# First block's mixer: the second query tile's attention tail split into three heads and one, both with priority

## The chip, the cores and the metric

One Trainium2 chip; the kernel runs on one of its cores. The metric is the device time of one execution in microseconds, the median over several runs.

## The reference

The program computes two transformer blocks one after the other: `first_block` (two layers, sequence of 256 tokens behind 16 meta tokens, 272 in all, width 1024) and `second_block` (two layers, whose norms are modulated by a vector made from a conditioning input `c`). Each layer of the first block has a mixer and a feed-forward part. The mixer, cut to what matters here:

```python
hn = rms_norm(h, norm_mix_g[l])
q, k, v, xr, gate = jnp.split(hn @ w_in[l], splits, axis=-1)
...
o_attn = diff_attention(q, k, v, lam)              # 4 heads, value width 128
o_attn = (rms_norm(o_attn, subln_g[l]) * (1.0 - lam_init)).reshape(B, T, D_ATTN)
o_rec = rg_lru_branch(xr, gate, conv_w[l], ...)    # conv, two gates, linear scan, gelu(gate)
o_rec = rms_norm(o_rec, rec_norm_g[l])
h = h + jnp.concatenate([o_attn, o_rec], axis=-1) @ w_out[l]
```

In `rg_lru_branch` the scan is over `a = exp(log_a)` and `u = sqrt(max(-expm1(2 log_a), 0)) * i * xc`, where `log_a` and `i` come from two 64x64 block matrices applied to the convolved `xc` (the gates).

## The kernel before, in words

All activations of the first block stay on the chip, channels on the partitions and the 272 tokens along the row. Every large product is made of three matmuls of split operands, high part by high part (line 359), low by high (360) and high by low (361). Weights come in blocks of 512 KB on SP's DMA queue (line 331); ScalarE copies the high part (336) and VectorE subtracts it to get the low part (337), three blocks ahead of their use.

`first_mixer` (line 612) projects q and k, normalizes them, projects v, and then runs the attention. `first_attend` (line 798) is a generator: for one tile of 128 queries it makes one head per step (scores, softmax on ScalarE and VectorE, transposes of the probabilities, the matmuls with v on lines 851 and 853 into the PSUM tile `po`), and after the last head it makes the tail: squares of `po` with a row sum on ScalarE (863), a small chain of reciprocal square root on VectorE (394 to 402, 865), the multiply that gives `on` (867), four transposes into the PSUM tile `pt` (871), the high part `mh` on ScalarE (878) and the low part `ml` on VectorE (879). Tile i=2 is the meta tokens (first layer only), i=0 and i=1 are the two halves of the sequence.

Between the heads' steps the recurrent branch is issued: `taps(c)` (convolution) and `gate(c)` for four chunks c of 128 channels. A gate has two matmuls into `pt` (741), each followed by a Tanh that reads it (742), then Tanh and Exp (743, 744). When the last gate is through, VectorE clips `th` (767), ScalarE takes its square root (768, which needs another function table to be loaded), and VectorE runs `recurrence(c)` (750 to 754, the scan is 753), adding squares into `rs` (423 to 427). `rstd_row` turns `rs` into a norm factor RR (matmul 437, the chain 394 to 402, matmul 446, copy 450), and lines 775 to 777 make `mh` and `ml` of chunks 4 to 7.

The output projection (781 to 796) has two halves of four weight blocks each: half 0 reads `mh`, `ml` of chunks 0 to 3, which are the attention, half 1 those of chunks 4 to 7, which are the recurrence. Line 791 adds each result to `h`. Into half 0 the steps of `ada_step` (469 on) are woven: the product of the conditioning vector with its weights `wada` (line 482, 128x32 by 32x256, four per 512 KB block), which come on POOL's queue (480) into five buffers. In the trace such a matmul leaves two records, so "x8" on line 482 or "x2" on line 741 is four matmuls, or one.

The order on each engine is the tile scheduler's: it walks the program in the order written, and what is issued under `high_priority(n)` is moved ahead by n. Each engine then runs its list in order, so an instruction that waits holds up all that stand behind it on that engine. PSUM buffers: `PSUM_BUFS` on line 39 gives acc 3, st 1, sc 2, pt 1, po 1; `pt` is shared by the gates' matmuls, the transposes of the probabilities and those of `on`.

Of the kernel before, what the change touches and what calls it, by code (L numbers as in the profile page):

```python
# [7 lines left out]
F32 = mybir.dt.float32  # L8
F32R = mybir.dt.float32r
I32 = mybir.dt.int32  # L10
AF = mybir.ActivationFunctionType
ALU = mybir.AluOpType
# [8 lines left out]
EPS = 1e-6  # L21
# [11 lines left out]
HP = 400  # L33
# [249 lines left out]
class Net:  # L283
# [514 lines left out]
    def first_attend(self, mp, l, i, qk, vn, aq, nlam, sub, mh, ml):  # L798

        nc = self.nc  # L800
        if i < 2:
            t0, nk = TILES[i][0], TILES[i][0] + 128
            mask = (self.m1, self.m2)[i]
            units = range(4)
        else:
            t0, nk, mask, units = 0, 16, self.m0, (0,)
        po = self.psum("po")
        rr = self.sp.tile([128, 4], F32, tag="rr", name="rr")
        for h in units:
            mx = self.sp.tile([128, 2], F32, tag="mx", name="mx")  # L810
            s = self.sp.tile([128, 2], F32, tag="sm", name="sm")
            p = []
            for c in range(2):
                r = slice(64 * c, 64 * c + 64)
                ps = self.psum("sc")
                if i < 2:
                    nc.tensor.matmul(ps[:, :nk], qk["q", h][r, t0:t0 + 128], qk["k", h][r, :nk], start=True, stop=True)
                    sc = aq[:, 16 * i + 8 + 2 * h + c:16 * i + 9 + 2 * h + c]
                else:
                    for hh in range(4):  # L820
                        nc.tensor.matmul(ps[32 * hh:32 * hh + 32, :16], qk["q", hh][r, 0:32], qk["k", hh][r, :16],
                                         start=True, stop=True, tile_position=(64 * c, 32 * hh))
                    sc = aq[:, 40 + c:41 + c]
                t = mp.tile([128, T], F32, tag=f"p{c}", name="p", bufs=2)[:, :nk]
                nc.vector.tensor_tensor_reduce(t, ps[:, :nk], mask, sc, -3e38, op0=ALU.add, op1=ALU.max,
                                               accum_out=mx[:, c:c + 1])
                p.append(t)
            nm = self.sp.tile([128, 2], F32, tag="nm", name="nm")
            nc.vector.tensor_scalar(nm, mx, -1.0, None, op0=ALU.mult)
            for c in range(2):  # L830
                nc.scalar.activation(p[c], p[c], AF.Exp, bias=nm[:, c:c + 1], accum_out=s[:, c:c + 1])
            r2 = self.sp.tile([128, 2], F32, tag="r2", name="r2")
            nc.vector.reciprocal(r2, s)
            nc.vector.tensor_copy(rr[:, h:h + 1], r2[:, 0:1])
            ra = self.sp.tile([128, 1], F32, tag="ra", name="ra")
            nc.vector.tensor_tensor(ra, s[:, 0:1], r2[:, 1:2], op=ALU.mult)
            nc.vector.tensor_tensor(ra, ra, nlam, op=ALU.mult)
            nc.vector.scalar_tensor_tensor(p[0], p[1], ra, p[0], op0=ALU.mult, op1=ALU.add)
            nt = nk // 128
            pt = self.psum("pt")  # L840
            nc.tensor.transpose(pt[0:16, 0:128], p[0][:, 0:16], self.idt)
            for j in range(nt):
                nc.tensor.transpose(pt[:, 128 + 128 * j:256 + 128 * j], p[0][:, 16 + 128 * j:144 + 128 * j], self.idt)
            am = mp.tile([16, 128], F32, tag="am", name="am", bufs=2)
            nc.scalar.activation(am, pt[0:16, 0:128], AF.Copy)
            if nt:
                a = mp.tile([128, 256], F32, tag="aT", name="aT", bufs=2)
                nc.scalar.activation(a[:, :128 * nt], pt[:, 128:128 + 128 * nt], AF.Copy)
            if i < 2:
                o = po[:, 128 * h:128 * h + 128]  # L850
                nc.tensor.matmul(o, am, vn[2][0:16, h], start=True, stop=False)
                for j in range(nt):
                    nc.tensor.matmul(o, a[:, 128 * j:128 * j + 128], vn[j][:, h], start=False, stop=j == nt - 1)
            else:
                for hh in range(4):
                    nc.tensor.matmul(po[32 * hh:32 * hh + 32, 0:128], am[:, 32 * hh:32 * hh + 32], vn[2][0:16, hh],
                                     start=True, stop=True, tile_position=(0, 32 * hh))
            yield
        n = len(units)
        so = self.sp.tile([128, 4], F32, tag="so", name="so")  # L860
        for h in units:
            junk = mp.tile([128, 128], F32, tag="junk", name="junk", bufs=2)
            nc.scalar.activation(junk, po[:, 128 * h:128 * h + 128], AF.Square, scale=rr[:, h:h + 1], accum_out=so[:, h:h + 1])
        y = self.rsqrt(so[:, :n], (128, n), 1.0 / 128, EPS, "ro")
        nc.vector.tensor_tensor(y, y, rr[:, :n], op=ALU.mult)
        on = mp.tile([128, 4, 128], F32, tag="on", name="on", bufs=2)[:, :n]
        nc.vector.tensor_tensor(on, po[:, :128 * n].rearrange("p (h e) -> p h e", h=n),
                                y.rearrange("p (h o) -> p h o", o=1).to_broadcast([128, n, 128]), op=ALU.mult)
        pt = self.psum("pt")
        for h in units:  # L870
            nc.tensor.transpose(pt[:, 128 * h:128 * h + 128], on[:, h], self.idt)
        if i < 2:
            src = pt.rearrange("p (h t) -> p h t", h=4)
            d = slice(t0, t0 + 128)
        else:
            src = pt[:, :128].rearrange("p (h t) -> p h t", h=4)[:, :, 0:16]
            d = slice(0, 16)
        nc.scalar.activation(mh[:, 0:4, d], src, AF.Copy, scale=sub)
        nc.vector.scalar_tensor_tensor(ml[:, 0:4, d], src, sub, mh[:, 0:4, d].bitcast(F32), op0=ALU.mult, op1=ALU.subtract)
        yield  # L880

    def gelu2(self, pool, out, x, n):
# [649 lines left out]
```

## Time and profile before

| | |
|---|---|
| median of 3 runs | 1718.66 us (1716.64 to 1721.53) |
| profiled execution: time | 1715.54 us |
| profiled execution: span | 1713.8 us |
| TensorE busy | 1654.7 us (97%) |
| VectorE busy | 1261.8 us (74%) |
| ScalarE busy | 848.1 us (49%) |
| mean granted TensorE clock | 0.982 |

All times below are microseconds from the start of the span, which begins 1.7 us or so later than the execution's own time counts. The mixer of the first layer is at about 60 to 160 us of it, that of the second at about 415 to 510. In the chain of waits and in the timelines, a bracket behind a row tells how long the engine was idle ahead of it and what released it.

### The profile page before, as it was taken

How to read it: one execution, taken by the hardware profiler on the slowest of the kernel's cores; microseconds unless marked ns; L12 is line 12 of the kernel's file. 1: busy time of each engine (PE TensorE's matmuls, PEld its weight loads, DVE VectorE, ACT ScalarE, POOL GpSimd, SP SyncE). 2: the span in 40 equal slices, each digit the busy share in tenths (PEclk: the TensorE clock that was granted, in tenths of full speed). 3: DMA queues.
4: the chain of work that ended last, by engine and by line, in shares of the span. 5: the costliest groups of instructions: out<-in, count | busy, mean ns of one | idle time of the engine just before them, and what ended most of it. 6: DMA issues, size and time to landing. Idle time of an engine off the chain costs nothing.

```text
span 1713.8 us, 27366 instructions
## 1 busy us (share of the span) xinstructions
PE 1654.7 (97%) x10336; PEld 1407.6 (82%) x10336; DVE 1261.8 (74%) x2713; ACT 848.1 (49%) x1614; POOL 71.2 (4%) x143
## 2 busy tenths in 40 slices
PE   8999999999989999999999999899999899979998
PEld 7869999998769999996667877677887786669997
DVE  7678986675887766745548898786867977687777
ACT  5575543454756444534556543133332846665554
POOL 0011000000000000000100011010100000000000
PEclk9999999999999999999999999899999999989999
DMA  7446655564356565432223355564642321146663
GB/s 267 157 156 233 217 172 172 166 188 152 101 189 191 184 185 185 143 99 74 72 71 99 111 170 192 163 201 140 215 161 85 119 75 38 62 119 186 186 185 112
DMA packets 71851, 256.77 MB, mean 150 GB/s; under 512 B 8584, under 2 KB 8600, under 8 KB 71720
## 3 DMA queue, kind: packets, MB, share of 16 engines
q1 hardware_dynamic: 56904, 203.58, 37.6%
q0 software_dynamic: 14672, 51.45, 9.2%
q8 instruction: 81, 1.33, 0.3%
q14 instruction: 50, 0.41, 0.1%
q10 hardware_dynamic: 144, 0.00, 0.0%
HBM read 253.92 MB, written 1.07 MB: 149 GB/s over the span
## 4 chain that ended last, share of the span: by engine, by line
PE 84%; DVE 7%; issue 5%; ACT 2%; DMA 1%; POOL 0%; DVEq 0%; POOLq 0%; ACTq 0%
PE acc L359 16%; PE acc L361 16%; PE acc L360 16%; PE up L361 6%; PE up L360 6%; PE up L359 6%; PE sc L1322 3%; PE y L359 2%; PE y L361 2%; PE y L360 2%; PE po L1333 2%; PE pt L1327 2%; DVE wlo L337 2%; PE st L533 1%; DVE asum L526 1%
## 5 line engine op out<-in xcount | busy, mean ns | idle before, releaser
L336 ACT ACTIVATE whi<-raw 128x1024 fp32r<-128x1024 f32 (+2 forms) x439 | 397.4, 919 | 544.7 <-PE acc L360 240.6
L337 DVE TENSOR_TENSOR wlo<-raw,whi 128x1024 fp32r<-128x1024 f32 (+2 forms) x439 | 457.4, 1050 | 204.9 <-ACT whi L336 196.8
L359 PE MATMUL acc<-hi,whi 128*128 128x272 f32 (+1 forms) x848 | 250.3, 295 | 7.8 <-ACT hi L567 7.2
L361 PE MATMUL acc<-hi,wlo 128*128 128x272 f32 (+1 forms) x848 | 248.1, 293 | 0.8 <-DVE wlo L337 0.8
L360 PE MATMUL acc<-lo,whi 128*128 128x272 f32 (+1 forms) x848 | 247.8, 292 | 0.0
L359 PEld LDWEIGHTS acc<-hi,whi 128*128 128x128 f32 x848 | 163.4, 193 | 15.3 <-ACT hi L567 7.2
L359 PE MATMUL acc<-whi,op 128*128 128x512 f32 (+1 forms) x432 | 157.0, 364 | 8.8 <-DVE y L1271 8.4
L360 PEld LDWEIGHTS acc<-lo,whi 128*128 128x128 f32 x848 | 163.4, 193 | 1.6 <-DVE lo L568 0.3
L361 PE MATMUL acc<-op,wlo 128*128 128x256 f32 (+1 forms) x528 | 164.7, 312 | 0.0
L360 PE MATMUL acc<-op,whi 128*128 128x256 f32 (+1 forms) x528 | 164.5, 312 | 0.2 <-DVE op L1072 0.2
L359 PE MATMUL acc<-op,whi 128*128 128x256 f32 (+1 forms) x528 | 164.4, 313 | 0.3 <-ACT qraw L1467 0.3
L361 PEld LDWEIGHTS acc<-hi,wlo 128*128 128x128 f32 x848 | 163.4, 193 | 1.2 <-DVE wlo L337 0.8
L360 PE MATMUL acc<-wlo,op 128*128 128x512 f32 (+1 forms) x432 | 155.2, 360 | 0.0
L360 PE MATMUL up<-op,whi 128*128 128x512 f32 (+1 forms) x384 | 146.2, 381 | 0.0
L359 PE MATMUL up<-op,whi 128*128 128x512 f32 (+1 forms) x384 | 145.6, 381 | 0.2 <-ACT pt L1070 0.2
L361 PE MATMUL up<-op,wlo 128*128 128x512 f32 (+1 forms) x384 | 145.0, 379 | 0.1
L359 PEld LDWEIGHTS acc<-op,whi 128*128 128x128 f32 x528 | 100.0, 190 | 8.7 <-issue 2.2
L360 PEld LDWEIGHTS acc<-op,whi 128*128 128x128 f32 x528 | 101.1, 192 | 6.6 <-issue 1.1
L526 DVE SCALAR_TENSOR_TENSOR asum<-wadb,csp,asum 128x1024 f32<-128x1024 f32 x84 | 104.4, 1277 | 2.1 <-DMA wadb<-wadb 2.1
L361 PEld LDWEIGHTS acc<-op,wlo 128*128 128x128 f32 x528 | 100.1, 190 | 6.3 <-issue 2.1
L359 PEld LDWEIGHTS acc<-whi,op 128*128 128x128 f32 x432 | 82.7, 192 | 25.9 <-DVE y L1271 8.8
L360 PEld LDWEIGHTS acc<-wlo,op 128*128 128x128 f32 x432 | 82.5, 191 | 12.2 <-issue 1.0
(416 smaller groups left out, 3389.9 us busy)
## 6 DMA issues: line engine op xcount, KB each, us to landing
raw<-wts SPq DMA_DIRECT2D x362, 512.0 KB, 3.7
wadb<-wadb POOLq DMA_DIRECT2D x64, 512.0 KB, 4.4
wada<-wada POOLq DMA_DIRECT2D x27, 512.0 KB, 5.6
raw<-wts SPq DMA_DIRECT2D x8, 384.0 KB, 3.1
B<-brow SPq DMA_DIRECT2D x6, 512.0 KB, 3.3
wada<-wada SPq DMA_DIRECT2D x5, 512.0 KB, 6.5
nb<-nbias POOLq DMA_DIRECT2D x16, 128.0 KB, 2.5
h<-xm SPq DMA_DIRECT2D x4, 272.0 KB
```

Of the source, the lines that this page charges most:

```text
L336: nc.scalar.activation(hi[:, cs], raw[:, cs], AF.Copy)
L337: nc.vector.tensor_tensor(lo[:, cs], raw[:, cs], hi[:, cs].bitcast(F32), op=ALU.subtract)
L359: mm(out, a[0], b[0], start=start, stop=False)
L360: mm(out, a[0], b[1], start=False, stop=False)
L361: mm(out, a[1], b[0], start=False, stop=stop)
L526: nc.vector.scalar_tensor_tensor(acc[s], w, c, acc[s], op0=ALU.mult, op1=ALU.add)
L533: nc.tensor.matmul(ps[:, 8 * s + m:8 * s + m + 1], acc[s][:, 128 * m:128 * m + 128], self.ones[:, 0:1], start=True, stop=True)
L1322: mm(ps[i], q[a][rows[i], tok], k[b][rows[i], k0:k0 + nk], start=n == 0, stop=n == 2)
L1327: nc.tensor.transpose(pt[:, 128 * j:128 * j + 128], p[:, 128 * j:128 * j + 128], self.idt)
L1333: mm(po[rows[i]], v[k0 // 128 + j][:, vc:vc + 64], pT[i][j // 2][:, 256 * (j % 2):256 * (j % 2) + 256], start=j == 0, stop=j == nj - 1, ti ...
```

## The change

The tail of `first_attend` becomes an inner function `finish(h0, h1)` that does the same for the heads h0 to h1 - 1. For tile i=1 it is called twice: `finish(0, 3)` after the last head's matmuls with v, and `finish(3, 4)` at the end, both under `high_priority(HP)` with HP = 400. For i=0 and i=2 it is called once, as before. The squares are now on line 816, the multiply with the factor on 819, `on` on 821, the transposes on 825, `mh` on 834 and `ml` on 835.

```diff
--- before.py
+++ after.py
@@ -806,6 +806,35 @@
             t0, nk, mask, units = 0, 16, self.m0, (0,)
         po = self.psum("po")
         rr = self.sp.tile([128, 4], F32, tag="rr", name="rr")
+
+        def finish(h0, h1):
+
+            n = h1 - h0
+            so = self.sp.tile([128, 4], F32, tag="so", name="so")
+            for h in range(h0, h1):
+                junk = mp.tile([128, 128], F32, tag="junk", name="junk", bufs=2)
+                nc.scalar.activation(junk, po[:, 128 * h:128 * h + 128], AF.Square, scale=rr[:, h:h + 1],
+                                     accum_out=so[:, h - h0:h - h0 + 1])
+            y = self.rsqrt(so[:, :n], (128, n), 1.0 / 128, EPS, "ro")
+            nc.vector.tensor_tensor(y, y, rr[:, h0:h1], op=ALU.mult)
+            on = mp.tile([128, 4, 128], F32, tag="on", name="on", bufs=2)[:, :n]
+            nc.vector.tensor_tensor(on, po[:, 128 * h0:128 * h1].rearrange("p (h e) -> p h e", h=n),
+                                    y.rearrange("p (h o) -> p h o", o=1).to_broadcast([128, n, 128]), op=ALU.mult)
+            pt = self.psum("pt")
+            for h in range(n):
+                nc.tensor.transpose(pt[:, 128 * h:128 * h + 128], on[:, h], self.idt)
+            if i < 2:
+                src = pt[:, :128 * n].rearrange("p (h t) -> p h t", h=n)
+                d = slice(t0, t0 + 128)
+                hs = slice(h0, h1)
+            else:
+                src = pt[:, :128].rearrange("p (h t) -> p h t", h=4)[:, :, 0:16]
+                d = slice(0, 16)
+                hs = slice(0, 4)
+            nc.scalar.activation(mh[:, hs, d], src, AF.Copy, scale=sub)
+            nc.vector.scalar_tensor_tensor(ml[:, hs, d], src, sub, mh[:, hs, d].bitcast(F32), op0=ALU.mult,
+                                           op1=ALU.subtract)
+
         for h in units:
             mx = self.sp.tile([128, 2], F32, tag="mx", name="mx")
             s = self.sp.tile([128, 2], F32, tag="sm", name="sm")
@@ -855,28 +884,18 @@
                 for hh in range(4):
                     nc.tensor.matmul(po[32 * hh:32 * hh + 32, 0:128], am[:, 32 * hh:32 * hh + 32], vn[2][0:16, hh],
                                      start=True, stop=True, tile_position=(0, 32 * hh))
+            if i == 1 and h == 3:
+                with self.tc.high_priority(HP):
+                    finish(0, 3)
             yield
-        n = len(units)
-        so = self.sp.tile([128, 4], F32, tag="so", name="so")
-        for h in units:
-            junk = mp.tile([128, 128], F32, tag="junk", name="junk", bufs=2)
-            nc.scalar.activation(junk, po[:, 128 * h:128 * h + 128], AF.Square, scale=rr[:, h:h + 1], accum_out=so[:, h:h + 1])
-        y = self.rsqrt(so[:, :n], (128, n), 1.0 / 128, EPS, "ro")
-        nc.vector.tensor_tensor(y, y, rr[:, :n], op=ALU.mult)
-        on = mp.tile([128, 4, 128], F32, tag="on", name="on", bufs=2)[:, :n]
-        nc.vector.tensor_tensor(on, po[:, :128 * n].rearrange("p (h e) -> p h e", h=n),
-                                y.rearrange("p (h o) -> p h o", o=1).to_broadcast([128, n, 128]), op=ALU.mult)
-        pt = self.psum("pt")
-        for h in units:
-            nc.tensor.transpose(pt[:, 128 * h:128 * h + 128], on[:, h], self.idt)
         if i < 2:
-            src = pt.rearrange("p (h t) -> p h t", h=4)
-            d = slice(t0, t0 + 128)
+            if i == 0:
+                finish(0, 4)
+            else:
+                with self.tc.high_priority(HP):
+                    finish(3, 4)
         else:
-            src = pt[:, :128].rearrange("p (h t) -> p h t", h=4)[:, :, 0:16]
-            d = slice(0, 16)
-        nc.scalar.activation(mh[:, 0:4, d], src, AF.Copy, scale=sub)
-        nc.vector.scalar_tensor_tensor(ml[:, 0:4, d], src, sub, mh[:, 0:4, d].bitcast(F32), op0=ALU.mult, op1=ALU.subtract)
+            finish(0, 1)
         yield
 
     def gelu2(self, pool, out, x, n):
```

How the scheduler's lists move is shown for the second layer's mixer, at the end of its attention. First TensorE. Before, from the last head's matmul with v (853) over the last gate's two matmuls (741) to the first matmuls of the projection (359 with whi); the rows of line 482 are the conditioning vector's:

```order
L853 MATMUL po<-vn_5014,aT 128x128
L741 MATMUL pt<-xc_5738,gates 128x272
L482 MATMUL acc<-wada,cs 32x256 x8
L741 MATMUL pt<-xc_5738,gates 128x272
L482 MATMUL acc<-wada,cs 32x256 x12
L871 MATMUL pt<-con_139,on 128x128 x4
L482 MATMUL acc<-wada,cs 32x256 x4
L359 MATMUL acc<-mh,whi_5628 128x256 x2
L482 MATMUL acc<-wada,cs 32x256 x3
```

The same place in the change:

```order
L882 MATMUL po<-vn_5034,aT 128x128
L482 MATMUL acc<-wada,cs 32x256 x15
L825 MATMUL pt<-con_139,on 128x128 x3
L482 MATMUL acc<-wada,cs 32x256 x4
L359 MATMUL acc<-mh,whi_5648 128x256 x2
L482 MATMUL acc<-wada,cs 32x256
L741 MATMUL pt<-xc_5758,gates 128x272
L360 MATMUL acc<-ml,whi_5648 128x256
L361 MATMUL acc<-mh,wlo_5649 128x256
L359 MATMUL acc<-mh,whi_5648 128x256
L360 MATMUL acc<-ml,whi_5648 128x256
L361 MATMUL acc<-mh,wlo_5649 128x256
```

The last gate's first matmul moved from directly behind line 853 to behind 20 matmuls of line 482, three transposes and two matmuls of the projection; its second follows after five more of the projection (and the last head's transpose after eight). In the first layer's mixer the list has 18, 3 and 1 matmuls of line 482 at these places.

Second ScalarE, at the same place, from the last gelu of the recurrent branch to the square root. Before:

```order
L888 ACTIVATE gl<-gl 128x272
L863 ACTIVATE junk,so<-po,rr 128x128 x2
L742 ACTIVATE tr<-pt,bh 128x272
L863 ACTIVATE junk,so<-po,rr 128x128
L743 ACTIVATE th<-tr,sp_4968 128x272
L863 ACTIVATE junk,so<-po,rr 128x128
L742 ACTIVATE ti<-pt,bh 128x272
L744 ACTIVATE tr<-tr,sp_4969 128x272
L768 ACT_TABLE_LOAD
L768 ACTIVATE th<-th 128x1088
L878 ACTIVATE mh<-pt,subg 128x4x128
```

And in the change:

```order
L907 ACTIVATE gl<-gl 128x272
L816 ACTIVATE junk,so<-po,rr 128x128 x4
L834 ACTIVATE mh<-pt,subg 128x3x128
L742 ACTIVATE tr<-pt,bh 128x272
L743 ACTIVATE th<-tr,sp_4988 128x272
L742 ACTIVATE ti<-pt,bh 128x272
L744 ACTIVATE tr<-tr,sp_4989 128x272
L834 ACTIVATE mh<-pt,subg 128x128
L768 ACT_TABLE_LOAD
L768 ACTIVATE th<-th 128x1088
```

All squares and `mh` of three heads now stand ahead of the gate's Tanh, and in this layer `mh` of the last head ahead of the table load (in the first layer it stands behind the square root). On VectorE `ml` moved from behind the first product of the recurrence (line 752) to ahead of the recurrence: three heads' within the second small chain, the last head's ahead of line 750.

## Rows read from the trace of the kernel before

**Rows 1.** The page's busy times: engine, busy us, share of the span, instructions.

```profile
PE 1654.7 (97%) x10336; PEld 1407.6 (82%) x10336; DVE 1261.8 (74%) x2713; ACT 848.1 (49%) x1614; POOL 71.2 (4%) x143
```

**Rows 2.** The page's chain that ended last, by engine.

```profile
PE 84%; DVE 7%; issue 5%; ACT 2%; DMA 1%; POOL 0%; DVEq 0%; POOLq 0%; ACTq 0%
```

**Rows 3.** TensorE's waits, 112 to 150 us: total us, times, longest.

```profile
PE acc L482 <- DMA wada<-wada: 1.5, 2, 0.8
PE acc L482 <- DVE th L750: 1.3, 1, 1.3
```

**Rows 4.** TensorE's waits, 465 to 510 us.

```profile
PE acc L482 <- DMA wada<-wada: 2.9, 2, 2.7
...
PE acc L359 <- ACT mh L776: 0.7, 1, 0.7
```

**Rows 5.** TensorE's waits, 146 to 300 us.

```profile
PE acc L359 <- DVE h L791: 0.4, 1, 0.4
```

**Rows 6.** Timeline, second mixer: start, us, engine, line, operation, out<-in, count [idle before].

```profile
470.94 0.62 PE L741 MATMUL pt<-xc,gates 128*128 128x272 f32 x2
...
471.14 0.37 ACT L863 ACTIVATE junk<-po,rr 128x128 f32<-128x128 f32 x1 [0.78 <-PE po L853]
...
475.71 1.11 ACT L768 ACTIVATE th<-th 128x1088 f32<-128x1088 f32 x1
...
476.88 0.98 PE L482 MATMUL acc<-wada,cs 128*32 128x256 f32 x8 [2.67 <-DMA wada<-wada]
...
478.09 1.06 PE L482 MATMUL acc<-wada,cs 128*32 128x256 f32 x2 [0.24 <-DMA wada<-wada]
...
480.95 0.75 DVE L879 SCALAR_TENSOR_TENSOR ml<-pt,subg,mh 128x512 fp32r<-128x512 f32 x1 [2.59 <-ACT mh L878]
...
488.52 1.22 DVE L337 TENSOR_TENSOR wlo<-raw,whi 128x1024 fp32r<-128x1024 f32 x1
...
490.15 0.83 PE L437 MATMUL st<-con,rs 128*128 128x1 f32 x6
...
499.49 0.62 PE L359 MATMUL acc<-mh,whi 128*128 128x256 f32 x3 [0.67 <-ACT mh L776]
```

**Rows 7.** Timeline, first mixer.

```profile
117.46 0.62 PE L741 MATMUL pt<-xc,gates 128*128 128x272 f32 x2
...
121.14 0.17 DVE L394 TENSOR_SCALAR rv<-so 128x4 f32<-128x4 f32 x1 [0.25 <-ACT junk L863]
...
121.40 0.64 PE L482 MATMUL acc<-wada,cs 128*32 128x256 f32 x8 [0.67 <-DMA wada<-wada]
...
122.42 1.11 ACT L768 ACTIVATE th<-th 128x1088 f32<-128x1088 f32 x1
...
123.12 0.69 DVE L867 TENSOR_TENSOR on<-po,ro 128x512 f32<-128x512 f32 x1
...
125.42 1.10 PE L871 MATMUL pt<-con,on 128*128 128x128 f32 x4
...
126.56 0.69 ACT L878 ACTIVATE mh<-pt,subg 128x512 fp32r<-128x512 f32 x1 [3.03 <-PE pt L871]
...
127.28 0.75 DVE L879 SCALAR_TENSOR_TENSOR ml<-pt,subg,mh 128x512 fp32r<-128x512 f32 x1 [1.29 <-ACT mh L878]
...
136.58 0.44 DVE L791 TENSOR_TENSOR h<-h,acc 128x272 f32<-128x272 f32 x1 [0.99 <-PE acc L361]
...
137.66 0.72 PE L437 MATMUL st<-con,rs 128*128 128x1 f32 x6
...
143.84 1.35 ACT L776 ACTIVATE mh<-xc,g 128x272 fp32r<-128x272 f32 x3 [0.51 <-DVE xc L775]
...
146.59 0.37 PE L359 MATMUL acc<-mh,whi 128*128 128x272 f32 x1 [0.37 <-DVE h L791]
```

**Rows 8.** Windows: us, busy of PE, PEld, DVE, ACT, POOL, granted clock, DMA share, GB/s.

```profile
125.00:129.00 4.00, 4.00 (x22) 1.79 (x21) 2.69 (x8) 1.12 (x2) 0.53 (x1) 0.57 1.00 401
498.00:499.00 1.00, 0.66 (x4) 0.42 (x4) 1.00 (x3) 0.20 (x2) 0.31 (x1) 1.00 0.93 356
```

## The prediction

> **What bounds the kernel now.** I read the page first. Its busy line shows TensorE at work in 97% of the span [rows 1], and the chain that ended last is TensorE for 84% of it [rows 2]; look there for the one engine whose time adds up to the whole. So nothing that VectorE or ScalarE gains or loses counts unless TensorE then waits less or more. Second, TensorE's waits in the two stretches that the change touches. In the first mixer they are 1.5 us for the c-vector's weights (wada) and 1.3 us where VectorE is late [rows 3]; in the second they are 2.9 us for wada and 0.7 us for mh of line 776, the first operand of the projection's second half [rows 4]. Between 146 and 300 us TensorE waits 0.4 us in all [rows 5], so whatever TensorE loses at the first mixer's second half is not made good behind it. Third, the timelines of both stretches, to see what stands between the last gate and that second half [rows 6, 7]. There lies the argument: the second half needs the recurrence, the recurrence needs the Sqrt of line 768, and Sqrt needs the last gate's matmuls of line 741. In the second mixer TensorE already waits for the end of this chain; in the first, the first mh (a third of the 1.35 us from 143.84) is written at 144.3 and the half starts at 146.59, so there are 2.3 us of room.
>
> **What moves.** The tail's eight squares, transposes and so on stay as many; per mixer the change adds a second chain of ten small VectorE operations (the chain took 121.14 to 123.12, so 1.98 us [rows 7]), one multiply, one ml and one mh. Alone that is about 3 us of VectorE and 0.4 of ScalarE per mixer, in gaps where VectorE waits 2.59 and 1.29 us for mh [rows 6, 7]; I cost it at nothing by itself. The c-vector's matmuls, their loads on POOL's queue and the weights' loads on SP's keep their number and, but for one weight load that goes ahead of a 4 KB store, their order.
>
> What counts is the order in front. TensorE's first gate matmul of the last step stood directly behind the last PV matmul; now 20 wada matmuls of the second mixer (15, 4 and 1) and three heads' transposes stand ahead of it. `pt` has one buffer, so it must also wait until ml of three heads has been read from it. On ScalarE the same: line 742 stood behind two squares, now behind four squares and mh of three heads.
>
> **Second mixer, step by step.** Before, the 20 wada matmuls that follow the gate are the same 20 (8 and 12 in the order): the last ones are released by their transfers at 476.88 (four) and 478.09 (the twentieth) [rows 6]. The transfers' pace does not depend on the new order, so the gate matmul cannot start before 478.1. The other branch: three squares of 0.37 from 471.14 end at 472.4; after 0.2 for the accumulator the small chain of 1.98 ends at 474.6; the multiply, by 384/512 of the 0.69 in rows 7, at 475.1; three transposes at 475.7; mh and ml by 3/4 of 0.69 and 0.75, with hand-overs, at 476.9. So the transfer comes last: the gate goes from 470.94 to about 478.2, **+7.2**. From the gate to the end of Sqrt took 5.9 us (470.94 to 475.71 + 1.11 [rows 6]); two squares of 0.37 leave it and mh of one head (about 0.35) comes in, so Sqrt ends +6.8. From there to the statistics matmul of line 437 at 490.15 VectorE took 13.3 us. Of this fall out the wait of 2.59 before ml and ml's 0.75 [rows 6], since ml is now done before Sqrt; in comes one more weight split in the list between, 1.22 [rows 6]. That leaves +4.7. Between line 437 and the second half there is one h add less (0.44, as in rows 7): **+4.3**, and since TensorE waits there already, all of it shows: the half starts near 503.8 instead of 499.49.
>
> **First mixer.** The next 18 wada matmuls stand ahead of the transposes; the fifteenth to eighteenth were released at 121.40 [rows 7], so TensorE is free at about 122.0. Squares, chain and multiply, worked as above, are ready at 121.7; four transposes took 1.10 with the clock low, three about 0.6 at the full clock; mh 0.55 and ml 0.55 end at 123.7. There `pt` comes free later than the second wait for wada in rows 3, and the gate starts at 123.7 instead of 117.46, **+6.2**; two squares less make it +5.5 at Sqrt (before: 122.42 + 1.11). To line 437 the 1.29 before ml goes, and 0.45 as ml covers one head instead of four; the 0.99 that VectorE waited for TensorE before an h add [rows 7] may go too, which gives +2.8 to +3.8. Two h adds of 0.44 then come before the norm: +3.6 to +4.6. Less the 2.3 of room that is +1.3 to +2.3. I take **+2**, and for the bounds 0.4 more to either side, about one small hand-over each: 0.9 to 2.7.
>
> **The early start** of the first half, the point of the edit, is costed at nothing: the time that TensorE saves ahead of half 0 it spends ahead of half 1. What is late next is the recurrence in both mixers.
>
> **Clock.** A price that the trace bounds only. [...] I take 0, as the gap in rows 8 is the nearest, and keep 3.4 for the range. [...]
>
> **Sum:** 4.3 + 2 = **+6.3**. The profiled execution took 1715.54 us, 3.1 below the median of 1718.66 (1716.64 to 1721.53); from it the sum gives 1721.8, from the median **1725.0**, which I give. About 0.3% (5.2 us) is what can be told from no change.
>
> **Rivals.** (a) *Faster, about 5.7 us (1713)*: the transposes of three heads fill TensorE's waits (1.5 + 1.3 and 2.9, rows 3, 4) and half 0 starts without them. It decides if the second mixer's gate starts before 473.4, since 2.5 us of delay is what the list behind it gives back by the working above. For it: VectorE's waits for mh go. Against: the twentieth matmul is released by a transfer at 478.09, and even without that transfer the three heads' chain ends at 476.9. [...] Chance 0.07.
> (b) *No change, +1 to +4 (1721)*: the scan catches up more than I count, since VectorE's list behind Sqrt has no foreign wait left; the first mixer's room then holds all and the second loses about 3. For it: 2.59 and 1.29 are the list's largest gaps. Chance 0.30.
> (c) *Slower by 8 to 12 (1728)*: the clock falls ahead of one or both second halves, or the gate's two matmuls themselves run at 0.50. Chance 0.18.
> (d) The change does not do what it says: the instruction order shows the split in both mixers and nowhere else; chance nil.
> My forecast, +4 to +8, has 0.45.
>
> **Numbers.** Range 1717 to 1732: it leaves out most of (a) and the far end of (c). Faster by over 0.3% needs (a): 0.07. Within 0.3%: (b) and the part of the forecast below +5.2, 0.30 + 0.05 = 0.35. Slower: 0.40 + 0.18 = 0.58.
>
> **What would show it.** In the changed profile: the gate's matmul (line 741) near 478 and 123.7; Sqrt's end near 483.6 and 129; TensorE's wait for mh of line 776 at 4 to 6 us in the second mixer and 1 to 3 in the first; no change from 160 to 455 us but a shift; the clock at 1.00 behind those waits. I am wrong if line 741 starts within 2 us of its old place, or if the second halves start no later than 146.6 and 499.5.

## The result, and the profile after

The changed kernel takes **1727.75 us** (median of 5 runs, 1726.30 to 1732.64) against 1716.64 us for the kernel before (5 runs, 1714.06 to 1721.53): a ratio of 1.0066, 95% interval 1.0043 to 1.0090, so some 11 us slower (7 to 15). The forecast was 1725.0, slower by 6.3, with a range of 1717 to 1732. The direction and the mechanism held; the size was taken too small.

The profiled execution took 1727.24 us, with a span of 1725.5 us; the span before was 1713.8. The page's busy times and its chain, which answer to [rows 1, 2]:

```profile
PE 1657.8 (96%) x10336; PEld 1411.6 (82%) x10336; DVE 1265.3 (73%) x2737; ACT 850.6 (49%) x1616; POOL 71.4 (4%) x143
```

```profile
PE 78%; issue 10%; DVE 7%; DMA 2%; ACT 2%; POOL 0%; DVEq 0%; POOLq 0%; SPq 0%; ACTq 0%
```

TensorE has as many instructions as before and 3 us more of busy time; the rest of the 11.7 us is time in which it stands still. VectorE has 24 instructions and 3.5 us more. TensorE's waits in the changed kernel, 100 to 160 us and then 440 to 520 us (total, times, longest), which answer to [rows 3, 4]:

```profile
PE acc L482 <- DMA wada<-wada: 3.7, 3, 2.7
PE st L446 <- DVE ry L402: 1.1, 1, 1.1
```

```profile
PE st L446 <- DVE ry L402: 3.7, 1, 3.7
PE acc L482 <- DMA wada<-wada: 2.9, 3, 1.6
PE acc L359 <- DVE h L791: 1.7, 1, 1.7
PE pt L825 <- DVE on L821: 1.4, 2, 1.1
```

The wait for the transfers is still there, 3.7 us in the first mixer (1.5 in [rows 3]) and 2.9 in the second (2.9 in [rows 4]). Longer than before are the waits ahead of line 446, the matmul of the recurrence's norm (before: none in the first mixer, 0.5 us in the second), and for `on` (before: 0.3 us). Look at the timeline of the second mixer, which answers to [rows 6] (start, us, engine, line, operation, and in brackets the idle time before and what ended it):

```profile
472.55 0.37 ACT L816 ACTIVATE junk<-po,rr 128x128 f32<-128x128 f32 x1 [0.77 <-PE po L882]
...
478.60 0.64 PE L482 MATMUL acc<-wada,cs 128*32 128x256 f32 x8 [1.64 <-DMA wada<-wada]
...
480.51 1.06 PE L482 MATMUL acc<-wada,cs 128*32 128x256 f32 x2 [0.62 <-DMA wada<-wada]
...
481.50 1.28 PE L741 MATMUL pt<-xc,gates 128*128 128x272 f32 x2
482.81 0.49 ACT L742 ACTIVATE tr<-pt,bh 128x272 f32<-128x272 f32 x1 [5.23 <-PE pt L741]
...
483.64 1.11 PE L741 MATMUL pt<-xc,gates 128*128 128x272 f32 x2
...
487.74 1.11 ACT L768 ACTIVATE th<-th 128x1088 f32<-128x1088 f32 x1
...
499.85 0.83 PE L437 MATMUL st<-con,rs 128*128 128x1 f32 x6
...
506.17 1.35 PE L446 MATMUL st<-con,ry 128*128 128x128 f32 x6 [3.73 <-DVE ry L402]
...
509.04 1.01 PE L359 MATMUL acc<-mh,whi 128*128 128x256 f32 x3
```

The first square starts at 472.55 instead of 471.14, so this execution enters the second mixer's tail 1.4 us late. The gate starts 10.6 us late, behind the twentieth wada matmul as forecast; the square root ends 12.0 us late (488.85), line 437 is 9.7 and half 1 9.55 us late. And in the first mixer, against [rows 7]:

```profile
121.75 0.64 PE L482 MATMUL acc<-wada,cs 128*32 128x256 f32 x8 [2.72 <-DMA wada<-wada]
...
124.62 0.73 PE L741 MATMUL pt<-xc,gates 128*128 128x272 f32 x2
...
128.85 1.11 ACT L768 ACTIVATE th<-th 128x1088 f32<-128x1088 f32 x1
...
141.02 0.72 PE L437 MATMUL st<-con,rs 128*128 128x1 f32 x6
...
146.59 1.00 PE L446 MATMUL st<-con,ry 128*128 128x128 f32 x6 [1.09 <-DVE ry L402]
```

The windows show what the forecast had left at nothing. Columns as in [rows 8]; the granted clock stands third from the end:

```profile
148.00:152.00 4.00, 3.92 (x18) 3.55 (x19) 3.62 (x13) 1.90 (x5) 2.32 (x5) 0.57 0.62 180
...
479.00:487.00 8.00, 7.38 (x34) 5.51 (x27) 2.04 (x6) 3.01 (x6) 0.00 (x0) 0.57 0.47 193
506.00:514.00 8.00, 7.34 (x35) 6.72 (x36) 4.78 (x13) 2.28 (x5) 1.59 (x3) 0.57 0.64 204
```

Three times TensorE has stood still and then runs at a mean of 0.57, once around the second mixer's gate and once into each half 1. But the kernel before has such stretches too (125 to 129 us in [rows 8]), so the mixers must be compared as a whole. The kernel before:

```profile
100.00:160.00 60.00, 56.72 (x429) 44.05 (x428) 47.70 (x135) 33.70 (x73) 9.44 (x18) 0.97 0.59 204
440.00:530.00 90.00, 82.22 (x633) 67.77 (x632) 75.85 (x223) 60.17 (x135) 5.26 (x10) 0.98 0.48 159
```

And the changed kernel:

```profile
100.00:160.00 60.00, 53.16 (x402) 41.76 (x401) 45.75 (x136) 32.02 (x69) 9.45 (x18) 0.97 0.60 206
440.00:530.00 90.00, 76.82 (x552) 62.35 (x551) 68.94 (x211) 51.83 (x122) 5.29 (x10) 0.92 0.44 146
```

TensorE stands still for 3.28 us in the first mixer before and for 6.84 us after (60.00 less its busy time), and for 7.78 and 13.18 us in the second. An estimate of what the lower clock costs, from these windows' mean clocks: it loses the same in the first mixer, 60 x 0.03 = 1.8 us, only at another place; in the second it loses 90 x 0.02 = 1.8 us before and 90 x 0.08 = 7.2 us after.

### The profile page after: what moved, and what is told of

It reads as the page before. It is cut to its first block, busy times and chain, and to the rows that moved or that the text cites. A ratio compares the mean times of both kernels' runs of the same rounds, so it can differ in the third digit from the quotient of the medians.

```text
span 1725.5 us, 27392 instructions
## 1 busy us (share of the span) xinstructions
PE 1657.8 (96%) x10336; PEld 1411.6 (82%) x10336; DVE 1265.3 (73%) x2737; ACT 850.6 (49%) x1616; POOL 71.4 (4%) x143
## 3 DMA queue, kind: packets, MB, share of 16 engines
q8 instruction: 81, 1.33, 0.3%
## 4 chain that ended last, share of the span: by engine, by line
PE 78%; issue 10%; DVE 7%; DMA 2%; ACT 2%; POOL 0%; DVEq 0%; POOLq 0%; SPq 0%; ACTq 0%
PE acc L359 15%; PE acc L360 14%; PE acc L361 14%; PE up L359 6%; PE up L361 6%; PE up L360 6%; PE sc L1341 3%; PE y L359 2%; PE y L361 2%; PE y L360 2%; PE po L1352 2%; PE pt L1346 2%; DVE wlo L337 2%; DMA wada<-wada 1%; PE st L533 1%
```

## The experiments

Theory **P**: `pt` has one buffer, and it is handed out in the order in which the program asks for it; `finish(0, 3)` asks before the last gate does, so the gate goes behind the transposes whatever the scheduler would like. Rivals: the priority did it (**S**), or the work added to VectorE (**V**). Each run was timed beside the kernel before on the same chip.

**1. The split without the priority.**

```diff
-                with self.tc.high_priority(HP):
-                    finish(0, 3)
+                finish(0, 3)
...
-                with self.tc.high_priority(HP):
-                    finish(3, 4)
+                finish(3, 4)
```

> Theory P (the one buffer of pt is handed out in the order in which the program asks for it; finish(0, 3) asks before the last gate, so the gate's matmuls go behind the three heads' transposes, whatever the priority): no change against the changed kernel, 9 to 13 us slower than the kernel before, line 741 near 124.6 and 481. Theory S (the priority moved the tail ahead of the gate): within 2 us of the kernel before, line 741 near 117.5 and 471. Theory V (the second small chain and the other work added to VectorE is what costs): as the changed kernel, but with line 741 at its old place.

Measured: 1729.96 us against 1719.58, ratio 1.0073 (1.0045 to 1.0100); line 741 at 126.21 and 483.44. As slow as the change, with the gate 1.6 and 2.4 us later than expected. The priority is not the cause.

**2. The priority without the split.** The whole tail as one `finish(0, 4)` at the end, under the priority.

```diff
-            if i == 1 and h == 3:
-                with self.tc.high_priority(HP):
-                    finish(0, 3)
...
-                    finish(3, 4)
+                    finish(0, 4)
```

> The whole tail in one piece behind the last gate, as before, but with the priority. Theory P: line 741 back at about 117.5 and 471; within 3 us of the kernel before, either way, since the tail's transposes and the recurrence only change places on VectorE. Theory S: 5 to 12 us slower. Theory V: within 2 us of before, as nothing is added.

Measured: 1718.44 us, ratio 0.9998 (0.9984 to 1.0012); line 741 at 116.32 and 470.62. As P has it: no loss, and no gain.

**3. The kernel before, with the last gate called after the tail.** No split, no priority, no added instruction.

```diff
-                if u < 4:
+                if u < 4 - i or u == 3 + i:
```

> The kernel before with one edit: the last gate is called after the whole tail, so that it asks for pt last. No split, no priority, no added instruction. Theory P: slower by 7 to 14 us, at least two thirds of what the change costs, with line 741 near 125 and 481 and the clock at 0.50 ahead of the second half. Theories S and V: within 2 us of the kernel before.

Measured: 1730.97 us, ratio 1.0075 (1.0048 to 1.0102). The timeline of the second mixer shows the gate's weight load (PEld, ahead of the matmul) released by the tail's `ml`, the last reader of `pt`:

```profile
487.70 0.30 PEld L741 LDWEIGHTS pt<-xc,gates 128*128 128x128 f32 x2 [0.41 <-DVE ml L879]
487.70 0.72 PE L741 MATMUL pt<-xc,gates 128*128 128x272 f32 x2
```

The order of asking alone makes a loss of this size, with nothing else of the change present. V is out as the main cause.

**4. The change, with both calls behind the last gate.** Split and priority stay.

```diff
-            if i == 1 and h == 3:
-                with self.tc.high_priority(HP):
-                    finish(0, 3)
...
             else:
+                with self.tc.high_priority(HP):
+                    finish(0, 3)
                 with self.tc.high_priority(HP):
                     finish(3, 4)
```

> The change's split and priority, but both calls stand behind the last gate, so that the gate asks for pt first. Theory P: line 741 at its old place, 4 us faster to 3 us slower than the kernel before. Theory V: 5 to 12 us slower, as all added work is there. Theory S: 5 to 12 us slower.

Measured: 1720.38 us, ratio 1.0005 (0.9986 to 1.0024). The gate is back at 116.88 and 469.12, and the loss is gone with all of VectorE's added work in place.

**5. The change, with the last gate one head earlier.**

```diff
-                if u < 4:
+                if u < 4 - i:
                     f, c = next(parts)
                     f(c)
+                if (i, u) == (1, 2):
+                    gate(3)
```

> The changed kernel with one edit: in the second tile the last gate is called one head earlier, so it asks for pt ahead of finish(0, 3). Split, priority and all added instructions stay. Theory P (order of asking for pt): the change's loss of 11 us goes; 3 us faster to 4 us slower than the kernel before, line 741's last pair ahead of the last head. Theory W (the order is only part of it; the chain of the split on VectorE and the low clock cost the larger share): still 5 us slower or more.

Measured: 1724.10 us against 1717.26, ratio 1.0054 (1.0031 to 1.0076): by its time this is what theory W of its expectation said. The gate itself is early (116.20), and the square root ends at 121.44 instead of 123.53. But look at ScalarE in the first mixer (the copy of line 876 is that of the last head's probabilities, `am<-pt`):

```profile
119.03 1.28 ACT L770 ACT_TABLE_LOAD   x1
...
120.33 1.11 ACT L770 ACTIVATE th<-th 128x1088 f32<-128x1088 f32 x1
121.34 0.25 ACT L876 ACTIVATE am<-pt 16x128 f32<-16x128 f32 x1
...
132.39 0.55 PE L827 MATMUL pt<-con,on 128*128 128x128 f32 x3 [2.19 <-DVE on L823]
```

With the gate ahead of the last head, the table load and the square root came ahead of that head's copies, and VectorE mixed the tail's small operations with the recurrence, so the three heads' transposes start at 132.39 instead of 122.33 in the change. No run isolates what this costs. Asking early enough is needed, but another chain pays when it is too early.

**6. to 8. The wada matmuls held back** until half 0's first h add: in the change (6), in the kernel before as a control (7), and in the kernel of run 4 (8). The edit is the same in all three:

```diff
                     nc.vector.tensor_tensor(self.h[:, c, oc], self.h[:, c, oc], ps, op=ALU.add)
+                    if (half, c) == (0, 0):
+                        cs = self.keep.tile([128, KD, 32], F32, name=f"cs{l}")
+                        nc.vector.scalar_tensor_tensor(cs.rearrange("p a b -> p (a b)"), self.h[:, 0, META:META + 256], 0.0,
+                                                       self.cs.rearrange("p a b -> p (a b)"), op0=ALU.mult, op1=ALU.add)
+                        self.cs = cs
```

> The changed kernel with the c-vector's matmuls held back until the first h add of half 0 (they read a copy of their operand that is made behind it), so no wada transfer can stand ahead of the gate. The gate stays behind three heads' transposes. Theory P with both waits: line 741 at about 477 instead of 481.5 in the second mixer and 123 to 124 in the first; the loss falls by 3 to 7 us to 3 to 8 us over the kernel before. If wada were the whole wait: within 2 us of the kernel before. If wada were no part of it: 9 to 13 us slower, as the changed kernel.

> The kernel before with the c-vector's matmuls held back in the same way, the control for the run beside it. TensorE's waits for wada ahead of half 0 (1.5 and 2.9 us) go, and the transfers have longer to land; but the 14 and 12 blocks then crowd into the rest of the projection. 6 us faster to 3 us slower than the kernel before.

> Both repairs on the change: its split and priority with the calls behind the last gate, and the c-vector's matmuls held back. Nothing of a transfer or of pt stands between the last head and half 0. Theory P: line 741 at its old place, half 0 at about 476 without a wait, 2 to 8 us faster than the kernel before. Theory V (the added VectorE work costs): no faster than the control.

Measured against 1717.26 us: 1731.58 (ratio 1.0084, 1.0069 to 1.0099), 1726.40 (1.0045, 1.0027 to 1.0062) and 1729.26 (1.0073, 1.0054 to 1.0093). All three expectations of the time failed. Run 8 is also 2.9 us slower than its control, run 7 (1727.4 to 1732.8 against 1722.7 to 1727.7), which is what its expectation gave as the sign of V. Runs 4 and 9, without this edit, speak against V, so why run 8 is no faster stays open. The control shows why the edit does not pay; its waits in 100 to 160 us, where the kernel before had 1.5 for wada and 1.3:

```profile
PE pt L876 <- DVE on L872: 4.2, 1, 4.2
PE po L856 <- ACT am L850: 1.0, 2, 0.6
```

The wada matmuls in front were the work that filled TensorE's wait for `on`; without them it stands still, and has them to do later. In run 6 the gate stands at 123.93 as expected, but at 487.07 in the second mixer, which that execution enters some 10 us late. As a repair the edit is of no use, but against its own control run 6 still tells something. From the second mixer's gate before the last (its second matmul) to the last gate it takes 6.05 us in the kernel before (464.89 to 470.94), 15.19 in the change (466.31 to 481.50), 11.74 in run 6 (475.33 to 487.07) and 5.47 in run 7 (471.92 to 477.39). So `pt` alone delays the gate by 6.3 us (11.74 - 5.47), and with the transfers in front it is 9.1 (15.19 - 6.05). And the change on top of the control costs 5.2 us (1731.58 - 1726.40), less than half of its 11.

**9. The change, with the second tile's transposes in other buffers.** Calls, split and priority as in the change.

```diff
-            pt = self.psum("pt")
+            pt = self.psum("sc" if i == 1 else "pt")
```

> The changed kernel with its calls where the change has them, split and priority kept, but the second tile's transposes go into the buffers of the scores (sc, two of them, idle after the last head) instead of the one of pt. Only who waits for pt differs. Theory P: line 741 back at its old place (117 and 471) and the time within 4 us of the kernel before. Theory W (what the call order or the added work does apart from the buffer): still 5 us slower or more.

Measured: 1717.98 us against 1717.93, ratio 0.9999 (0.9984 to 1.0014). The gate is at 117.84 and, in the timeline of the second mixer,

```profile
467.80 0.62 PE L741 MATMUL pt<-xc,gates 128*128 128x272 f32 x2
...
474.20 1.08 PE L482 MATMUL acc<-wada,cs 128*32 128x256 f32 x8 [3.12 <-DMA wada<-wada]
475.21 0.90 PE L825 MATMUL sc<-con,on 128*128 128x128 f32 x3
...
477.10 0.58 PE L359 MATMUL acc<-mh,whi 128*128 128x256 f32 x1
...
496.87 0.39 PE L359 MATMUL acc<-mh,whi 128*128 128x256 f32 x1 [0.37 <-ACT mh L776]
```

6.04 us behind the gate before it (461.76), as before. One name of a buffer takes the whole 11 us back: this settles P. It also shows what the split is worth when nothing is in its way. From the gate, half 0 starts after 9.30 us instead of 10.03 (470.94 to 480.97 before), since three transposes still stand behind a transfer of wada, and half 1 after 29.07 instead of 28.55. Nothing that can be measured.

**10. and 11. The change in one layer's mixer only.**

```diff
-            if i == 1 and h == 3:
+            if i == 1 and h == 3 and l == 0:
...
-            if i == 0:
+            if i == 0 or l == 1:
```

(and the mirror of it, with l == 1 and l == 0, for run 11).

> The change in the first layer's mixer alone. By the two traces the mixer ends 3.0 us later: 1 to 4 us slower than the kernel before, the second mixer with line 741 0.2 us behind its last head as before. If the low clock passed on to later stages, more than 5.

> The change in the second layer's mixer alone. By the two traces that mixer loses 9.7 us: 7 to 11 us slower than the kernel before. With the run beside it the two losses should add up to the change's 11 within 3 us; if the mixers' losses depended on each other, they would not.

Measured against 1717.93 us: 1723.62 (ratio 1.0029, 1.0018 to 1.0039; 5.0 us, 3.1 to 6.7) and 1725.55 (1.0039, 1.0024 to 1.0053; 6.7 us, 4.1 to 9.1). They add up to 11.7 us against the change's own 11, as expected, so within these intervals neither loss depends on the other. Each loss by itself missed its expectation (1 to 4 and 7 to 11), and the split is nearer to 5 and 7 than to the 3.0 and 9.7 that the two traces gave. Which split is right stays open, as the traces of these runs repeat the other split. Take the time between two matmuls of TensorE, the same two in each run, which stand at 100 and 165 us and at 440 and 540 us in the kernel before. The first mixer takes 65.02 us there, 68.26 in the change and 68.25 in run 10; the second takes 99.94, 109.56 and, in run 11, 109.44. But the mixer that a run leaves as it was also takes 1.0 us more than in the trace of the kernel before (66.01 in run 11, 101.05 in run 10), so that one trace is a yardstick to about a microsecond only.

## Why the prediction was right, and where it was short

The loss of some 11 us lies outside the forecast's +4 to +8 and inside rival (c), +8 to +12, which had a chance of 0.18 and named what came on top: the clock ahead of half 1 and on the gate's own matmuls. That the time itself was missed by only 2.75 us (1727.75 against 1725.0) is in part luck: the forecast was laid on a median of 1718.66, and with two runs more the kernel before has 1716.64.

- *The gate falls behind the transposes and the transfers*: right, in both mixers, and the cause was named with both parts, one buffer of `pt` and the wada matmuls. Runs 3 and 9 show the first as necessary and, with the wada matmuls in place, enough; runs 6 and 7 measure it at 6.3 of the 9.1 us in the second mixer. The prediction's own branch without the transfers, 476.9 against 470.94, made 6.0.
- *First mixer's gate at 123.7, Sqrt's end at 129, line 437 +2.8 to +3.8, the half 2 us late*: measured 124.62, 129.96, +3.4 (141.02 against 137.66), and 2.5 us at the start of half 1 (149.11 against 146.59), which is 3.0 at its end. Right within a microsecond in this trace. The timed run 10 gives this mixer more, 5.0 us (3.1 to 6.7) against a forecast of 2 and an upper bound of 2.7; where the rest of it arises is not shown.
- *Second mixer, gate +7.2*: +9.1 once the late entry of 1.4 us is taken off. The transfers did not keep their times: the twentieth matmul is released at 480.51, 2.4 us later than in [rows 6] instead of 1.4, and at a clock of 0.50 that matmul itself holds the gate for 1.0 us (480.51 to 481.50).
- *Sqrt +6.8*: +10.6. From gate to square root's end it took 7.35 us (481.50 to 488.85) where 5.5 was worked out, mainly because the gate's two matmuls ran at a granted clock of 0.50, 1.28 and 1.11 us, where at 1.00 in the kernel before the first took 0.62 [rows 6] and the second 0.73; and `mh` of the last head put the table load off by 0.7 us where 0.35 was counted.
- *From Sqrt to line 437, 11.2 us*: 11.0 (488.85 to 499.85). The working on VectorE's list was right, and so was the stretch from line 437 to half 1 (8.9 forecast, 9.2 measured, 499.85 to 509.04).
- *Clock, taken at 0, bounds 0 to 3.4*: **this is the term that failed.** The 3.4 was the author's estimate, twice the 4 x 0.43 of 125 to 129 us in [rows 8], and no run shows it as the bound. In its place the changed kernel's windows give, by the same estimate, 4 x 0.43 = 1.7 us for 148 to 152 and 8 x 0.43 = 3.4 us each for 479 to 487 and 506 to 514. Less what the kernel before loses in the same mixers (1.8 and 1.8), the price is by estimate about 5 us (8.5 less 3.6; 5.4 by the mixers' mean clocks), some of it beside waiting. All of it is in the second mixer, 3.4 us in half 1 and the rest around the gate, where the sum had no term. In the first mixer nothing was added: the stretch at 125 to 129 us is gone, and the one at 148 to 152 stands in its place. Neither row of [rows 8] could tell this. In the kernel before the wait of 2.67 us that ends at 476.88 [rows 6] is followed by a clock of 0.50 from 478 to 480 us; in the change the wait of 2.72 us that ends at 121.75 is not, and the clock is 1.00 from 120 to 148 us. So the length of a wait did not tell here whether a low stretch comes behind it. No run isolates the clock's share.
- *Time that TensorE stands still*, which is what the sum of 6.3 forecast: also short. It grew by 3.6 us in the first mixer (3.28 to 6.84) and by 5.4 in the second (7.78 to 13.18), 9.0 together. In the second the later transfer and the slow gate above are what the trace shows for it; in the first the excess is not explained.
- *What would show it*: the waits were named for mh of line 776; they stand ahead of that, at line 446, and are shorter (3.7 and 1.1 us against 4 to 6 and 1 to 3), as TensorE's list has the norm's matmul ahead of half 1.
- *The split's added work at nothing*: right; runs 4 and 9 carry all of it and come out at 1.0005 and 0.9999.
- *Rival (a), faster once the gate is in place*: even with the gate in place (runs 4 and 9) nothing is gained, as in the second mixer the three transposes still stand behind a transfer of wada, for which TensorE waits 2.50 us in run 4 and 3.12 in run 9.

## What to carry to other kernels

Where several producers share one rotating buffer, the place of the call in the program set their order here, and the priority did not undo it (runs 1 to 4); before moving a piece of work earlier, look which shared buffer it asks for, and who asks next. A chain that feeds a later stage can be the one that is put off when an earlier stage is hurried. And some of TensorE's waits here had a low clock behind them: a wait of 3.73 us was followed by a mean of 0.57 (506 to 514 us in the changed kernel), and of two waits of about 2.7 us one was followed by 0.50 (478 to 480 us in the kernel before) and one by 1.00 (from 121.75 us in the changed kernel). So give that price a range at every place where the change brings a wait, and take off what the kernel before already pays.

## What the runs showed of the hardware that was not expected

The granted clock was 0.91 in one execution and 1.00 in another over the same stretch, in which the profile shows TensorE never idle in either. It is the window of 400 to 420 us, which the change doesn't touch, in the kernel before and in the changed one:

```profile
400.00:420.00 20.00, 20.00 (x134) 17.24 (x133) 10.56 (x26) 8.48 (x18) 0.53 (x1) 0.91 0.45 131
```

```profile
400.00:420.00 20.00, 20.00 (x144) 17.07 (x144) 10.96 (x26) 8.57 (x17) 0.53 (x1) 1.00 0.48 151
```

0.91 over 20 us is by estimate 1.8 us (20 x 0.09) lost in one execution and not in the other. This is most of how the first mixer's delay of 3.0 us shrank to 1.4 us at the entry of the second: ahead of that stretch a matmul of line 711 starts 2.73 us late in the change (411.81 against 409.08), and behind it the third one after that is 1.33 us late (417.89 against 416.56). It lies between the two mixers, so it does not explain why their shares in single traces (3.0 and 9.7) differ from those of the timed runs (5.0 and 6.7). Its cause is not known.
